# Laying inputs channel-major and weights in 4 KB pieces, without input transposes on TensorE

## The chip, the cores and the metric

The kernel runs on one core of a Trainium2 chip. The metric is the device time in microseconds (us) of one execution; smaller is better. Of the core's engines, TensorE multiplies matrices (PE in the profile, with its weight loads as PEld), VectorE (DVE) and ScalarE (ACT) work element by element, GpSimd (POOL) does little here, and SyncE (SP) issues nearly all transfers (DMAs).

## The reference

One layer of a decoder trunk, for T = 320 token rows (256 of a prompt, and 8 samples of 8 tokens) of D = 2048 channels:

```
h = RMSNorm(x) * norm_mix_g
B_a, C_a, v_a, glu_a, glu_b, gate_a, gate_b = split(h @ w_in)        # 7 x 2048 columns
y_a = (B_a * causal_conv3(C_a * v_a)) @ w_out_a
u   = glu_a * sigmoid(glu_b)
y_b = silu(LayerNorm(causal_conv31(u) + bias)) @ w_out_b
x   = x + (sigmoid(gate_a) * y_a + sigmoid(gate_b) * y_b) @ w_o
x   = x + (silu(n(x) @ w_gate) * (n(x) @ w_up)) @ w_down             # n: RMSNorm, 5632 hidden columns
y   = RMSNorm(x) * final_norm_g
```

Both convolutions also take past rows (state_conv_a, state_conv_b) for the samples and return the new last rows. All inputs and outputs are float32.

## The kernel before

Activations are held channel-major: a chunk c is a tile of 128 channels by 320 tokens, and there are 16 of them. A weight piece is 512 rows by 256 columns (512 KB, `raw`). It is split into a high part `whi` (a cast to fp32r on ScalarE, L207) and a low part `wlo` (raw minus whi on VectorE, L208); activations have such parts too (`rh`/`rl`, `hh`/`hl`). Each product is three matmuls of 128x320: high by high (L244), high weight by low activation (L245), low weight by high activation (L246). A unit is 256 output columns, so one piece is 4 rows of k times 2 accumulators times 3 = 24 matmuls, and a unit of 2048 rows has four pieces.

The first three units (glu_b, glu_a, glu_b again) run as a group (`run_group`): r counts the four pieces of each unit, m the three units, k the four chunks of a piece. In the group, and in the three units after it, the activation is x times the norm's gain, without the norm's factor per token; the factor `rb` is multiplied in when these accumulators are evicted. `at_start(r, m, k)` says what is issued ahead of which step of the group. `x_chunk` turns the token-major x into chunk c by three transposes on TensorE (`px`), then makes `rh`, `rl` and the plain copy `xc`. `x_squares` and `x_factor` make the norm's factor per token row, and `x_spread` spreads it over the partitions by three small matmuls (`rps`). `x_norm(c)` makes the normalized chunk for the later units, and writes `xc` to a scratch tensor, from which `post_o` reads it again. The parameters are turned by `turn_params` (`pp`), the conv states by `turn_state_b` (`sT`) and `turn_state_a` (`aT`), the new rows on their way out in `post_ga` (`uT`) and `rows_a` (`vT`). Twelve matmuls on zeros (`spin`, L92) run while the first loads arrive.

Order: within each engine and queue instructions run in the order in which they were put there by a scheduler from the program's order; `issue_after` holds an instruction behind another. Weight loads go out four pieces ahead of use into five buffers, splits run one piece ahead in the group and two later (three buffers).

Of the kernel before, what the change touches and what calls it, by code (L numbers as in the profile page):

```python
# [38 lines left out]
def trunk_kernel(ctx: ExitStack, tc: tile.TileContext, a):  # L39
# [33 lines left out]
    xpair, xt = rows3("xt")
    xpv = a["x_prompt"][0].rearrange("(i p) d -> p i d", p=P)

    def load_x(c0, c1, queues):
        hs = slice(c0 * P, c1 * P)
        queues[0].dma_start(out=xpair[:, :, hs], in_=xpv[:, :, hs])
# [3 lines left out]
    nc.gpsimd.memset(xt[2][TS:P, :], 0.0)
# [8 lines left out]
    for _ in range(12):  # L91
        first = te.matmul(o[:, :T], idle[:, 0:P], idle, start=True, stop=True, skip_group_check=True).ins  # L92
# [6 lines left out]
    ac.activation(out=warm, in_=ones[:, 0:1], func=AF.Sigmoid)  # L99

    gmix = const.tile([P, NC], F32, name="gmix")
    with tc.issue_after(first):
        pp = pst("pp")
        te.transpose(out=pp[:, 0:NC], in_=grow, identity=ident[:NC, :NC])
    gm = ve.tensor_copy(out=gmix, in_=pp[:, 0:NC]).ins

    prow = const.tile([P, 5, P], F32, name="prow")
    prm = const.tile([P, 5 * P], F32, name="prm")

    def load_params():  # L110
        with tc.issue_after(last_load[0].ins):
            fetch_params()

    def fetch_params():
        r0 = 16
        for n, rows in (("norm_ffn_g", 16), ("conv_b_bias", 16), ("ln_b_g", 16), ("ln_b_b", 16)):
            nc.sync.dma_start(out=prow[r0 : r0 + rows, 0, :], in_=a[n].rearrange("o (c p) -> (o c) p", p=P))
            r0 += rows
        nc.sync.dma_start(out=prow[0:16, 0, :], in_=a["final_norm_g"].rearrange("(c p) -> c p", p=P))
        nc.sync.dma_start(out=prow[80:128, 0, :], in_=a["conv_a_w"].rearrange("o j (c p) -> (o j c) p", p=P))  # L120
        cbv = a["conv_b_w"].rearrange("o j (c p) -> (o j c) p", p=P)
        nc.sync.dma_start(out=prow[:, 1:4, :], in_=cbv[0:384].rearrange("(t q) p -> q t p", q=P))
        nc.sync.dma_start(out=prow[0:112, 4, :], in_=cbv[384:496])

    def turn_params():
        with tc.issue_after(last_mm[0]):
            pp = pst("pp")
            for t in range(4):
                te.transpose(out=pp[:, t * P : (t + 1) * P], in_=prow[:, t, :], identity=ident)
            ve.tensor_copy(out=prm[:, 0:512], in_=pp)  # L130
            pp = pst("pp")
            last_mm[0] = te.transpose(out=pp[:, 0:112], in_=prow[0:112, 4, :], identity=ident[:112, :112]).ins
            ve.tensor_copy(out=prm[:, 512:624], in_=pp[:, 0:112])
# [39 lines left out]
    last_load = [None]  # L173
    nsplit = [0]

    def load_to(i):
        while nload[0] <= min(i, len(pieces) - 1):
            q = pieces[nload[0]]
            n, nb = q["n"], q["nb"]
            r = wp.tile([P, KP, NB], F32, tag="raw", bufs=RAW_BUFS, name=nm("raw"))  # L180
            step = 2 if nload[0] == 0 else n
            for k in range(0, n, step):
                r0 = (q["k0"] + k) * P
                last_load[0] = nc.sync.dma_start(
                    out=r[:, k : k + step, :nb],
                    in_=q["w"][r0 : r0 + step * P, q["n0"] : q["n0"] + nb].rearrange("(k p) n -> p k n", p=P),
                )
# [4 lines left out]

    def split_to(i):
        while nsplit[0] <= min(i, len(pieces) - 1):
# [6 lines left out]
            if nsplit[0]:  # L201
                split(q, 0, n)
            nsplit[0] += 1

    def split(q, k0, k1):
        ks, nb = slice(k0, k1), q["nb"]
        ac.copy(out=q["hi"][:, ks, :nb], in_=q["raw"][:, ks, :nb])  # L207
        ve.tensor_tensor(  # L208
            out=q["lo"][:, ks, :nb], in0=q["raw"][:, ks, :nb], in1=q["hi"][:, ks, :nb].bitcast(F32), op=ALU.subtract
        )  # L210
# [110 lines left out]
    xc = [None] * NC  # L321
# [4 lines left out]
    def x_chunk(c):  # L326
        px = pst("px")
        with tc.issue_after(last_mm[0]):
            for i, (t0, _) in enumerate(blk):
                last_mm[0] = te.transpose(  # L330
                    out=px[:, t0 : t0 + P], in_=xt[i][:, c * P : (c + 1) * P], identity=ident
                ).ins
        r_hi[c] = slot("rh", F32R)
        r_lo[c] = slot("rl", F32R)
        x_last["ac"] = ac.activation(out=r_hi[c], in_=px[:, :T], func=AF.Copy, scale=g_mix(c)).ins
        x_last["ve"] = ve.scalar_tensor_tensor(
            out=r_lo[c], in0=px[:, :T], scalar=g_mix(c), in1=r_hi[c].bitcast(F32), op0=ALU.mult, op1=ALU.subtract
        ).ins
        xc[c] = slot("xc")
        if c % 2:  # L340
            ve.tensor_copy(out=xc[c], in_=px[:, :T])
        else:
            ac.copy(out=xc[c], in_=px[:, :T])

    def x_squares(q):

        with tc.issue_after(x_last["ve"]), tc.issue_after(x_last["ac"]):
            for i in range(3):
                v = xt[i][:, q * 4 * P : (q + 1) * 4 * P]
                if i == 1:  # L350
                    ve.scalar_tensor_tensor(
                        out=v, in0=v, scalar=1.0, in1=v, op0=ALU.mult, op1=ALU.mult, accum_out=sq4[:, i, q : q + 1]
                    )
                else:
                    ac.activation(out=v, in_=v, func=AF.Square, accum_out=sq4[:, i, q : q + 1])

    def x_factor():
        ve.tensor_reduce(out=ss, in_=sq4, axis=mybir.AxisListType.X, op=ALU.add)
        ve.tensor_scalar(out=ss, in0=ss, scalar1=1.0 / D, scalar2=RMS_EPS, op0=ALU.mult, op1=ALU.add)
        rsqrt(ss, rst, rtmp, (P, 3))  # L360

    def x_spread():
        rps = pst("rps")
        dg = []
        for i in range(3):
            dg.append(slot("dg", shape=(P, P)))
            ve.tensor_scalar(out=dg[i], in0=ident, scalar1=rst[:, i : i + 1], scalar2=None, op0=ALU.mult)
        with tc.issue_after(last_mm[0]):
            for i, (t0, n) in enumerate(blk):
                last_mm[0] = te.matmul(  # L370
                    rps[:, t0 : t0 + n], ones, dg[i][:, :n], start=(i == 0), stop=(i == 2), skip_group_check=True
                ).ins
        ve.tensor_copy(out=rb, in_=rps[:, :T])
# [11 lines left out]
    lnacc = sm.tile([P, T], F32, name="lnacc")  # L385


    mid = []

    def load_states(b):  # L390

        if not mid:
            mid.extend((io.tile([P, 2, D], F32, tag="pair", name=nm("win")), io.tile([P, D], F32, tag="one", name=nm("stb"))))
        sbv = a["state_conv_b"].rearrange("o b j d -> (o b j) d").rearrange("(i r) d -> r i d", i=2)
        with tc.issue_after(last_load[0].ins):
            nc.sync.dma_start(out=stb(b)[:120], in_=sbv[:, :, b * NB : (b + 1) * NB])

    def stb(b):
        return mid[1].rearrange("p (g i n) -> p g i n", g=4, i=2)[:, b % 4]
# [11 lines left out]
    ex = [None] * NC  # L411

    def conv_b_tasks(c, up):
# [4 lines left out]
        def first():  # L418
            w = mid[0][:, c % 2, : (T // SS) * 40].rearrange("p (g k) -> p g k", k=40)
# [37 lines left out]
    def turn_state_b(c):  # L457
        pt = pst("sT")
        with tc.issue_after(last_mm[0]):
            for i in range(2):  # L460
                last_mm[0] = te.transpose(  # L461
                    out=pt[:, i * 120 : (i + 1) * 120], in_=stb(c // 2)[:120, i, (c % 2) * P : (c % 2 + 1) * P], identity=ident[:120, :120]
                ).ins
        ex[c] = slot("ext", shape=(P, SB, WB - 1))
        ac.copy(out=ex[c], in_=pt[:, 0:240].rearrange("p (b j) -> p b j", b=SB))

# [562 lines left out]
```

## Time and profile before

| | |
|---|---|
| median of 3 runs | 2098.7 us (2097.35 to 2098.91) |
| profiled execution, its own time | 2099.18 us |
| its span, first to last instruction | 2097.4 us |
| mean granted TensorE clock | 0.999 |
| TensorE busy | 2085.0 us |
| VectorE, ScalarE, GpSimd busy | 1268.7, 822.7, 6.0 us |
| transfers | 323.81 MB, mean 154 GB/s |

In a row of the timeline stand start, duration, engine, line, operation, written tile <- read tiles, shapes, count, and in brackets the idle time before it and what ended it. In the chain stand start, the time that the step takes on the chain, and engine, tile and line. A row of groups ends with total busy us, mean ns of one, and the idle time before them. A row of windows has the stretch, then per engine the busy us and the instructions, then the granted clock, the DMA share and GB/s. TensorE's matmuls are pipelined, so that their durations overlap: what one costs is the distance of two starts.

### The profile page before, as it was taken

The page shows a single profiled execution, that of the slowest core. Times are in us where ns is not written, and L with a number is a line of the kernel's source. Part 1 is how long each engine was busy: PE and PEld are TensorE (multiplying, and loading weights), DVE is VectorE, ACT ScalarE, POOL GpSimd, SP SyncE. Part 2 cuts the span into 40 slices and gives each one's busy share as a digit, 9 for nine tenths or more (in the row PEclk, how much of TensorE's full clock was granted, in tenths as well). Part 3 has the DMA queues.
Part 4 walks back from the last instruction along what each step waited for, and adds up shares of the span by engine and source line. Part 5 has one row for each costly group of instructions (what it writes and reads, how often), then busy time and mean ns, then how long its engine had stood idle before and what let it go on. Part 6 is the DMA issues. An engine that isn't in the chain of part 4 may idle for free.

```text
span 2097.4 us, 34309 instructions
## 1 busy us (share of the span) xinstructions
PE 2085.0 (99%) x14245; PEld 2080.9 (99%) x14245; DVE 1268.7 (60%) x1859; ACT 822.7 (39%) x1245; POOL 6.0 (0%) x24
## 2 busy tenths in 40 slices
PE   9999999999999999999999999999999999999998
PEld 8999999999999999999999999999999999999998
DVE  6888789988987754335555654455333545544444
ACT  5544444444434444333344333333223333333443
POOL 0000000000000000000000000000000000000000
PEclk9999999999999999999999999999999999999999
DMA  8654544444444444444455444444444444444443
GB/s 245 191 167 151 181 150 148 149 149 150 152 151 149 144 153 149 151 151 151 154 173 170 148 150 151 151 151 146 146 155 153 148 149 150 151 151 146 149 141 111
DMA packets 321289, 323.81 MB, mean 154 GB/s; under 512 B 11134, under 2 KB 318862, under 8 KB 321102
## 3 DMA queue, kind: packets, MB, share of 16 engines
q1 hardware_dynamic: 321022, 321.56, 48.1%
q8 instruction: 111, 1.82, 0.3%
q14 instruction: 44, 0.36, 0.0%
q10 hardware_dynamic: 112, 0.07, 0.0%
HBM read 315.42 MB, written 7.60 MB: 154 GB/s over the span
## 4 chain that ended last, share of the span: by engine, by line
PE 99%; DVE 0%; ACT 0%; DMA 0%; issue 0%; SPq 0%; ACTq 0%; DVEq 0%
PE acc L244 32%; PE acc L246 32%; PE acc L245 32%; PE acc L797 0%; PE acc L795 0%; PE acc L796 0%; PE ya L750 0%; DMA raw<-in_w_in 0%; PE px L330 0%; ACT whi L207 0%; PE sT L461 0%; PE acc L801 0%; PE acc L800 0%; DVE wlo L208 0%; PE uT L477 0%
## 5 line engine op out<-in xcount | busy, mean ns | idle before, releaser
L208 DVE TENSOR_TENSOR wlo<-raw,whi 128x1024 fp32r<-128x1024 f32 (+1 forms) x593 | 716.4, 1208 | 713.3 <-ACT whi L207 710.0
L207 ACT CAST whi<-raw 128x1024 fp32r<-128x1024 f32 (+1 forms) x593 | 614.4, 1037 | 1157.1 <-PE acc L245 896.8
L244 PE MATMUL acc<-hh,whi 128*128 128x320 f32 x1600 | 495.2, 310 | 0.0
L246 PE MATMUL acc<-hh,wlo 128*128 128x320 f32 x1600 | 494.5, 309 | 0.0
L245 PE MATMUL acc<-hl,whi 128*128 128x320 f32 x1600 | 494.3, 309 | 0.0
L245 PE MATMUL acc<-gl,whi 128*128 128x320 f32 x1408 | 435.3, 309 | 0.0
L244 PE MATMUL acc<-gh,whi 128*128 128x320 f32 x1408 | 435.1, 309 | 0.0
L246 PE MATMUL acc<-gh,wlo 128*128 128x320 f32 x1408 | 435.1, 309 | 0.0
L245 PEld LDWEIGHTS acc<-hl,whi 128*128 128x128 f32 x1600 | 300.3, 188 | 0.1
L244 PEld LDWEIGHTS acc<-hh,whi 128*128 128x128 f32 x1600 | 300.2, 188 | 0.2
L246 PEld LDWEIGHTS acc<-hh,wlo 128*128 128x128 f32 x1600 | 300.2, 188 | 0.1
L433 DVE SCALAR_TENSOR_TENSOR cb<-win,prm,cb 128x320 f32<-128x320 f32 x480 | 259.4, 549 | 9.1 <-ACT cb L429 1.0
L245 PEld LDWEIGHTS acc<-gl,whi 128*128 128x128 f32 x1408 | 264.3, 188 | 0.1
L246 PEld LDWEIGHTS acc<-gh,wlo 128*128 128x128 f32 x1408 | 264.3, 188 | 0.1
L244 PEld LDWEIGHTS acc<-gh,whi 128*128 128x128 f32 x1408 | 264.3, 188 | 0.0
L246 PE MATMUL acc<-fh,wlo 128*128 128x320 f32 x660 | 204.4, 310 | 0.0
L244 PE MATMUL acc<-fh,whi 128*128 128x320 f32 x660 | 204.1, 309 | 0.0
L245 PE MATMUL acc<-fl,whi 128*128 128x320 f32 x660 | 203.9, 309 | 0.0
L244 PEld LDWEIGHTS acc<-fh,whi 128*128 128x128 f32 x660 | 123.9, 188 | 0.0
L246 PEld LDWEIGHTS acc<-fh,wlo 128*128 128x128 f32 x660 | 123.9, 188 | 0.0
L245 PEld LDWEIGHTS acc<-fl,whi 128*128 128x128 f32 x660 | 123.9, 188 | 0.0
L244 PE MATMUL acc<-ah,whi 128*128 128x320 f32 x256 | 79.3, 310 | 0.0
(187 smaller groups left out, 2105.0 us busy)
## 6 DMA issues: line engine op xcount, KB each, us to landing
raw<-in_w_in SPq DMA_DIRECT2D x223, 512.0 KB, 3.5
raw<-in_w_gate SPq DMA_DIRECT2D x88, 512.0 KB, 3.5
raw<-in_w_up SPq DMA_DIRECT2D x88, 512.0 KB
raw<-in_w_down SPq DMA_DIRECT2D x80, 512.0 KB, 3.3
raw<-in_w_out_a SPq DMA_DIRECT2D x32, 512.0 KB
raw<-in_w_out_b SPq DMA_DIRECT2D x32, 512.0 KB, 3.3
raw<-in_w_o SPq DMA_DIRECT2D x32, 512.0 KB, 3.3
raw<-in_w_down SPq DMA_DIRECT2D x16, 256.0 KB, 2.8
```

The costliest lines, as they stand in the source:

```text
L207: ac.copy(out=q["hi"][:, ks, :nb], in_=q["raw"][:, ks, :nb])
L208: ve.tensor_tensor(out=q["lo"][:, ks, :nb], in0=q["raw"][:, ks, :nb], in1=q["hi"][:, ks, :nb].bitcast(F32), op=ALU.subtract)
L244: te.matmul(o, wh, hi[kk], start=(kk == 0), stop=False)
L245: te.matmul(o, wh, lo[kk], start=False, stop=False)
L246: return te.matmul(o, wl, hi[kk], start=False, stop=(kk == nk - 1)).ins
L433: ve.scalar_tensor_tensor(out=o, in0=win[0][:, :, j + 2 : j + 10], scalar=w_cb(j, c), in1=o, op0=ALU.mult, op1=ALU.add)
```

## The change

Before the launch, numpy now lays x, the parameters and the conv states channel-major, with the norm's gain in front of the first chunk (`lead`), and the weights so that each of a piece's 128 partitions reads one run of 4 KB where it read four of 1 KB. Two outputs leave the core channel-major and are laid out by numpy afterwards. All transposes of inputs on TensorE are gone, and those of the new conv rows; the transposes of y at the end stay. The scratch copy of x is gone: `post_o` reads the input again. The squares of the first norm are taken per chunk on ScalarE, summed over the 16 chunks on GpSimd (`lnacc`), and one matmul with ones sums over the partitions and gives every partition the sum; the factor is then computed on 128x320 tiles, with ScalarE's square root and VectorE's reciprocal. The first weight piece comes in three transfers, two of them on ScalarE's queue; the second is split in halves. Nine matmuls on zeros remain.

```
-    for _ in range(12):
+    for _ in range(9):
         first = te.matmul(o[:, :T], idle[:, 0:P], idle, start=True, stop=True, skip_group_check=True).ins
...
+    lead = const.tile([P, NC + T], F32, name="lead")
+    gmix, xc[0] = lead[:, 0:NC], lead[:, NC : NC + T]
+    sp.dma_start(out=lead, in_=a["x"][:, 0 : NC + T])
+    def load_x(cs):
+        for c in cs:
+            xc[c] = slot("xc")
+            sp.dma_start(out=xc[c], in_=xcol(c))
...
-            step = 2 if nload[0] == 0 else n
...
+            ks = (0, 1, 2, n) if nload[0] == 0 else (0, n)
+            for k, k1 in zip(ks, ks[1:]):
+                eng = aq if nload[0] == 0 and k < 2 else sp
+                dm = eng.dma_start(out=r[:, k:k1, :], in_=q["w"][q["n0"] // NB, :, q["k0"] + k : q["k0"] + k1, :])
...
     def x_chunk(c):
-        px = pst("px")
-        with tc.issue_after(last_mm[0]):
-            for i, (t0, _) in enumerate(blk):
-                last_mm[0] = te.transpose(
-                    out=px[:, t0 : t0 + P], in_=xt[i][:, c * P : (c + 1) * P], identity=ident
-                ).ins
...
+        x_last["ac"] = ac.activation(out=r_hi[c], in_=xc[c], func=AF.Copy, scale=g_mix(c)).ins
         x_last["ve"] = ve.scalar_tensor_tensor(
+            out=r_lo[c], in0=xc[c], scalar=g_mix(c), in1=r_hi[c].bitcast(F32), op0=ALU.mult, op1=ALU.subtract
         ).ins
+    def x_square(c):
+        q = slot("sq")
+        ac.activation(out=q, in_=xc[c], func=AF.Square)
+        if c == 0:
+            nc.gpsimd.tensor_copy(out=lnacc, in_=q)
         else:
+            nc.gpsimd.tensor_tensor(out=lnacc, in0=lnacc, in1=q, op=ALU.add)
     def x_factor():
+        p = pst("rps")
         with tc.issue_after(last_mm[0]):
+            last_mm[0] = te.matmul(p[:, :T], ones, lnacc, start=True, stop=True).ins
+        ve.tensor_scalar(out=lnv, in0=p[:, :T], scalar1=1.0 / D, scalar2=RMS_EPS, op0=ALU.mult, op1=ALU.add)
+        ac.activation(out=lnr, in_=lnv, func=AF.Sqrt)
+        ac.activation(out=warm, in_=lnr[:, 0:1], func=AF.Sigmoid)
+        ve.reciprocal(out=rb, in_=lnr)
+        ve.tensor_tensor(out=lnt, in0=lnv, in1=rb, op=ALU.mult)
+        ve.scalar_tensor_tensor(out=lnt, in0=lnt, scalar=-0.5, in1=rb, op0=ALU.mult, op1=ALU.mult)
+        ve.scalar_tensor_tensor(out=rb, in0=lnt, scalar=1.5, in1=rb, op0=ALU.add, op1=ALU.mult)
     def x_norm(c):
-        with tc.issue_after(last_load[0].ins):
-            nc.sync.dma_start(out=xs[c], in_=xc[c])
...
-                pt = pst("uT")
-                te.transpose(out=pt[: WB - 1 + TS, 0:P], in_=up[:, TP - (WB - 1) : T], identity=ident)
-                ac.copy(out=uo[:, j * P : (j + 1) * P], in_=pt[: WB - 1 + TS, 0:P])
+                nc.sync.dma_start(out=a["nb_new"][c], in_=up[:, TP - (WB - 1) : T])
...
+        elif 3 * r + m <= 7:
+            x_square(6 * r + 2 * m - 2 + k // 2 if k % 2 == 0 else 14 + k // 2)
...
+        elif (r, m, k) == (2, 2, 3):
+            x_factor()
...
+    load_x((1, 2, 3))
+    split_to(0)
+    after_load[1, 0] = lambda: load_x((4, 5))
+    after_load[2, 0] = lambda: load_x((6, 7))
```

Three places show what moves. The first is the start of SyncE's queue. `xt` are the token-major x tiles, `raw` a weight piece, `lead` and `xc` chunks of x. Before:

```order
L78 DMA xt_76<-in_x_prompt 128x2x256
L184 DMA raw_133<-in_w_in 128x2x256
L78 DMA xt_76<-in_x_prompt 128x2x256
L79 DMA xt_77<-in_x_sample 64x256
L184 DMA raw_133<-in_w_in 128x2x256
L184 DMA raw_138<-in_w_in 128x4x256
L184 DMA raw_140<-in_w_in 128x4x256
L78 DMA xt_76<-in_x_prompt 128x2x512
```

And now:

```order
L77 DMA lead<-in_x 128x336
L85 DMA xc_108<-in_x 128x320
L85 DMA xc_110<-in_x 128x320
L85 DMA xc_112<-in_x 128x320
L155 DMA raw_114<-in_w_in 128x512
L155 DMA raw_127<-in_w_in 128x1024
L85 DMA xc_129<-in_x 128x320
L85 DMA xc_131<-in_x 128x320
L155 DMA raw_133<-in_w_in 128x1024
```

Two chunks of x now stand behind each whole piece, and the first half of the first piece (`raw_114`) has moved to ScalarE's queue.

The second is TensorE's queue in the ninth piece of the group (r = 2, m = 2), where the norm's sum is made. `acc` is an accumulator, `rps` the sum's tile, `dg` the factors on a diagonal. Before:

```order
L244 MATMUL acc_132<-rh_368,whi_553 128x320
L245 MATMUL acc_132<-rl_369,whi_553 128x320
L246 MATMUL acc_132<-rh_368,wlo_554 128x320
L370 MATMUL rps_610<-dg_611,ones 128x128
L370 MATMUL rps_610<-dg_613,ones 128x128
L370 MATMUL rps_610<-dg_615,ones 128x64
L244 MATMUL acc_131<-rh_398,whi_553 128x320
```

And now:

```order
L229 MATMUL acc_126<-rl_367,whi_492 128x320
L230 MATMUL acc_126<-rh_366,wlo_493 128x320
L329 MATMUL rps_553<-lnacc,ones 128x320
L228 MATMUL acc_125<-rh_385,whi_492 128x320
L229 MATMUL acc_125<-rl_386,whi_492 128x320
```

One matmul on GpSimd's sum stands in the place of three on VectorE's factors, six matmuls of the stream further down.

The third is ScalarE's queue ahead of that piece's cast (`whi_553` before, `whi_492` now). Before:

```order
L207 CAST whi_487<-raw_324 128x1024
L335 ACTIVATE rh_501<-px_497,gmix 128x320
L343 COPY xc_505<-px_497 128x320
L335 ACTIVATE rh_523<-px_519,gmix 128x320
L355 ACTIVATE xt_76,sq_117<-xt_76 128x512
L355 ACTIVATE xt_77,sq_117<-xt_77 128x512
L207 CAST whi_553<-raw_380 128x1024
```

And now:

```order
L188 CAST whi_448<-raw_301 128x1024
L320 ACTIVATE sq_468<-xc_149 128x320
L313 ACTIVATE rh_477<-xc_257,lead 128x320
L320 ACTIVATE sq_489<-xc_207 128x320
L320 ACTIVATE sq_502<-xc_255 128x320
L320 ACTIVATE sq_511<-xc_209 128x320
L320 ACTIVATE sq_520<-xc_257 128x320
L188 CAST whi_492<-raw_345 128x1024
```

The last four squares (`sq`), each of which GpSimd adds in turn, stand together there, where two sums over token rows stood.

More of the change, by code (lines that the diff above doesn't have):

```diff
@@ L98, in trunk_kernel @@
     warm = const.tile([P, 1], F32, name="warm")
[L99 to L107, printed above, removed]
     prm = const.tile([P, 5 * P], F32, name="prm")
@@ L111, in load_params @@
         with tc.issue_after(last_load[0].ins):
[L112 to L125, printed above, removed]
-        with tc.issue_after(last_mm[0]):
[L127 to L133, printed above, removed]
+            nc.sync.dma_start(out=prm[:, 0:624], in_=a["prm"])
     def col(i):
@@ L200, in split_to @@
             q["hi"], q["lo"] = h, l
-            if nsplit[0]:
+            if nsplit[0] == 1:
+                split(q, 0, 2)
+                split(q, 2, 4)
+            elif nsplit[0]:
                 split(q, 0, n)
@@ L205, in split, with hi_part, lo_part @@
     def split(q, k0, k1):
[L206 to L210, printed above, removed]
+        hi_part(q, k0, k1)
+        lo_part(q, k0, k1)
+    def hi_part(q, k0, k1):
+        ks = slice(k0, k1)
+        if q is pieces[0] and k0 == 0:
+            return ve.tensor_copy(out=q["hi"][:, ks, :], in_=q["raw"][:, ks, :]).ins
+        return ac.copy(out=q["hi"][:, ks, :], in_=q["raw"][:, ks, :]).ins
+    def lo_part(q, k0, k1):
+        ks = slice(k0, k1)
+        return ve.tensor_tensor(
+            out=q["lo"][:, ks, :], in0=q["raw"][:, ks, :], in1=q["hi"][:, ks, :].bitcast(F32), op=ALU.subtract
+        ).ins
     late = []
@@ L320, in trunk_kernel @@
     rb = sm.tile([P, T], F32, name="rb")
-    xc = [None] * NC
+    lnacc = sm.tile([P, T], F32, name="lnacc")
+    lnv = sm.tile([P, T], F32, name="lnv")
+    lnr = sm.tile([P, T], F32, name="lnr")
+    lnt = sm.tile([P, T], F32, name="lnt")
     x_last = {}
@@ L357, in x_factor @@
-    def x_factor():
[L358 to L367, printed above, removed]
-        with tc.issue_after(last_mm[0]):
[L369 to L373, printed above, removed]
+    def x_square(c):
[3 more added lines that the diff above has]
+            nc.gpsimd.tensor_copy(out=lnacc, in_=q)
+        else:
+            nc.gpsimd.tensor_tensor(out=lnacc, in0=lnacc, in1=q, op=ALU.add)
@@ L383, in trunk_kernel @@
     acts_h = lambda: (h_hi, h_lo)
-    lnacc = sm.tile([P, T], F32, name="lnacc")
-    mid = []
+    win_ = [None]
+    ex = [None] * NC
     def load_states(b):
[L392 to L399, printed above, removed]
+        if win_[0] is None:
+            win_[0] = io.tile([P, 2, D], F32, tag="pair", name=nm("win"))
+        for c in (2 * b, 2 * b + 1):
+            ex[c] = slot("ext", shape=(P, SB, WB - 1))
+            with tc.issue_after(last_load[0].ins):
+                nc.sync.dma_start(out=ex[c], in_=a["sb"][c])
     def states_through():
         with tc.issue_after(last_load[0].ins):
-            nc.sync.dma_start(out=a["new_b_s"][0, :, 0 : WB - 1 - SS, :], in_=a["state_conv_b"][0, :, SS : WB - 1, :])
-    w_in = a["w_in"][0]
+            nc.sync.dma_start(out=a["nb_old"], in_=a["state_conv_b"][0, :, SS : WB - 1, :])
+    w_in = a["w_in"]
     O_B, O_C, O_V, O_GA, O_GB, O_SA, O_SB = (i * D for i in range(7))
@@ L455, in post_gb @@
         return f
[L457 to L465, printed above, removed]
     def post_ga(b, raw):
         def f(acc):
-            uo = slot("uo", shape=(WB - 1 + TS, NB))
             for j in range(2):
@@ L1018 @@
     arrays, args = {}, {}
-    for name in _INS:
-        x = _np.ascontiguousarray(inputs[name])
+    for name, x in _lay_in(_np, inputs).items():
         arrays[f"in_{name}"] = x
```

223 lines of the change are left out of this document (84 added, 139 removed).

## The prediction

> **What bounds the kernel now.** I read the busy line and the chain of the page first.
>
> ```profile
> PE 2085.0 (99%) x14245; PEld 2080.9 (99%) x14245; DVE 1268.7 (60%) x1859; ACT 822.7 (39%) x1245; POOL 6.0 (0%) x24
> PE 99%; DVE 0%; ACT 0%; DMA 0%; issue 0%; SPq 0%; ACTq 0%; DVEq 0%
> ```
>
> TensorE is busy in 2085 of 2097.4 us and is 99% of the chain. Work taken off another engine is worth nothing by itself; what counts is TensorE time removed, or TensorE gaps. So next come the shares of the chain over the first 300 us, which hold nearly all transposes that the change touches.
>
> ```profile
> by line: PE acc L246 29.9%; PE acc L244 29.8%; PE acc L245 29.7%; DMA raw<-in_w_in 1.6%; PE px L330 1.3%; ACT whi L207 1.2%; PE sT L461 1.1%; DVE wlo L208 0.8%; issue 0.6%; PE uT L477 0.6%; DVE rl L336 0.4%; ACT rh L335 0.3%; SPq L78 0.3%;
> ```
>
> Of 300 us the transposes of x (px) hold 3.9 us, of the conv state (sT) 3.3, of u (uT) 1.8. About 5% is no matmul: the head, and one stall. TensorE's timeline gives the price of one transposed chunk:
>
> ```profile
> 20.18 0.31 PE L246 MATMUL acc<-rh,wlo 128*128 128x320 f32 x1
> 20.33 0.49 PE L330 MATMUL px<-ident,xt 128*128 128x128 f32 x3
> 20.58 0.39 PE L244 MATMUL acc<-rh,whi 128*128 128x320 f32 x1
> 20.81 0.30 PE L245 MATMUL acc<-rl,whi 128*128 128x320 f32 x1
> ...
> 21.39 0.31 PE L246 MATMUL acc<-rh,wlo 128*128 128x320 f32 x1
> 21.53 0.31 PE L244 MATMUL acc<-rh,whi 128*128 128x320 f32 x1
> ```
>
> Undisturbed matmuls start 0.146 us apart (20.81 to 21.39 is four steps of 0.145); their 0.31 us overlap. From 20.33 to 20.81 stand one matmul and three transposes: 0.48 - 0.146 = 0.33 us for a chunk. The last row is the first matmul of the fourth weight piece: 72 main matmuls are over at 21.53. The stall:
>
> ```profile
> 43.30 0.31 PE L246 MATMUL acc<-rh,wlo 128*128 128x320 f32 x1
> 46.08 0.85 PE L370 MATMUL rps<-dg,ones 128*128 128x128 f32 x6 [2.47 <-DVE dg L367]
> 46.74 0.44 PE L244 MATMUL acc<-rh,whi 128*128 128x320 f32 x1
> 46.98 0.47 PE L245 MATMUL acc<-rl,whi 128*128 128x320 f32 x1
> ...
> 50.18 0.40 PE L245 MATMUL acc<-rl,whi 128*128 128x320 f32 x1
> 50.42 0.31 PE L246 MATMUL acc<-rh,wlo 128*128 128x320 f32 x1
> ```
>
> TensorE waits 2.47 us for the small vector chain of the first norm, and then runs 14 matmuls at 0.27 us apart, about half speed, until 50.42.
>
> **The change, part by part.**
>
> *The norm stall.* 43.30 to 50.42 is 7.12 us and holds 15 matmul steps, 15 x 0.146 = 2.2 us: it costs 4.9. The new x_factor puts one fp32 matmul of ones with lnacc there. The same form stands later in the chain, at 0.54 us:
>
> ```profile
> 658.49 0.54 PE mu L588 x2
> ```
>
> If lnacc is ready, 4.9 - 0.5 = 4.4 us are saved. Its readiness is the question of the GpSimd adds, below.
>
> *Transposes after the fourth piece.* Eight of the sixteen x chunks are turned there: 8 x 0.33 = 2.7 us. sT 3.3 and uT 1.8 go wholly (rows above). The parameters and the state of mixer A:
>
> ```profile
> 51.16 0.44 PE pp L129 x4
> 51.60 0.10 PE pp L132
> 263.70 0.22 PE aT L511 x2
> ```
>
> That is 0.54 + 0.22; the three vT transposes I put at uT's 1.8/16 = 0.1 each. Sum 8.9 us, all on the path, since TensorE is the chain. The evictions that go with them (ACT and VectorE) and the 16 scratch writes by SP gain nothing: nobody on the path waits for them. New on SP are 16 stores of `up`, where loads queue behind a wait for VectorE instead of ACT; the loads have cover, since their wait is for free buffers:
>
> ```profile
> SPq L184 <- DVE wlo L208: 1347.0, 451, 7.4
> DMA packets 321289, 323.81 MB, mean 154 GB/s; under 512 B 11134, under 2 KB 318862, under 8 KB 321102
> ```
>
> Those rows also value the 4 KB pieces at nothing after the head: weights wait for room, not TensorE for weights, and 154 GB/s are used where the head below moves 300. Were that cover gone, a late load would cost its lateness. The other queue edits go with it: one load of parameters for eight, sixteen of states for eight, one of mixer A's state for sixteen, one store of its new rows for six; all on SP, between weight loads that wait for room.
>
> *The head.* Its limits are the transfers.
>
> ```profile
> 0.00:4.00 4.00, 2.75 (x10) 2.75 (x11) 0.33 (x1) 1.49 (x2) 2.64 (x8) 1.00 0.41 131
> 4.00:8.00 4.00, 3.35 (x16) 2.08 (x15) 1.42 (x3) 1.47 (x3) 0.00 (x0) 1.00 1.07 307
> 8.00:12.00 4.00, 3.69 (x23) 2.80 (x21) 2.63 (x6) 3.05 (x7) 0.00 (x0) 1.00 1.08 319
> 6.94 0.56 PE L244 MATMUL acc<-rh,whi 128*128 128x320 f32 x2 [0.29 <-ACT rh L335]
> 7.67 0.62 ACT L207 CAST whi<-raw 128x512 fp32r<-128x512 f32 x1 [0.79 <-DMA raw<-in_w_in]
> ```
>
> The last two columns are DMA share and GB/s: saturated from 4 us on, at 307 to 319 GB/s, after 0.52 MB by 4 us. The second half of the first piece ends 1.18 MB of issues; those bytes have moved at 4 + 0.66/0.307 = 6.1 us, and its user starts at 7.67: 1.5 us of lag. Now the new order. Ahead of the second piece's end stand lead 0.17, three chunks 0.49, and two pieces 1.05: 1.71 MB, moved at 7.9, landed at 9.4. It is split in halves; ACT takes 0.62 (row above) and VectorE about 0.6 for one, so its low part allows the third matmul at 10.7 and the piece ends 22 x 0.146 later, at 13.9. The third piece ends 2.57 MB: moved at 10.7, landed 12.2, then whi and wlo:
>
> ```profile
> L208 DVE TENSOR_TENSOR wlo<-raw,whi 128x1024 fp32r<-128x1024 f32 (+1 forms) x593 | 716.4, 1208 | 713.3 <-ACT whi L207 710.0
> L207 ACT CAST whi<-raw 128x1024 fp32r<-128x1024 f32 (+1 forms) x593 | 614.4, 1037 | 1157.1 <-PE acc L245 896.8 <-issue 233.7 <-ACT win L426 5.8
> L672 DVE SCALAR_TENSOR_TENSOR gl<-x,prm,gh 128x320 fp32r<-128x320 f32 x16 | 8.7, 545 | 0.0
> L671 ACT ACTIVATE gh<-x,prm 128x320 fp32r<-128x320 f32 x16 | 8.9, 558 | 0.0
> L675 ACT ACTIVATE sq<-x 128x320 f32<-128x320 f32 x16 | 7.3, 457 | 0.0
> L312 DVE TENSOR_TENSOR lnacc<-lnacc,sq 128x320 f32<-128x320 f32 x43 | 21.0, 488 | 1.3
> L82 POOL MEMSET xt<- 64x2048 f32 x1 | 1.8, 1800 | 0.3 <-POOLq L1017 0.3
> L99 ACT ACT_TABLE_LOAD x1 | 1.3, 1283 | 1.8 <-issue 1.8
> L847 DVE RECIPROCAL rst<-rtmp x3: 149/155/157, 2084.9 to 2091.3; 128x1 f32<-128x1 f32 x2, 64x1 f32<-64x1 f32 x1
> 1.25 3.57 PE L92 MATMUL spin<-idle 128*128 128x320 f32 x12 [1.25 <-DVE idle L89]
> 2089.92 0.44 DVE yt L835
> ```
>
> 12.2 + 1.04 + 1.21 = 14.4, and 22 matmuls later, at 17.6, the 72 are done, against 21.53: 3.9 us saved, the four px of that stretch (1.3) among them. The bounds: lead and the first half of the first piece, 0.43 MB, have moved at 3.7 and landed at 5.2, so a first matmul comes at 5.8 behind ACT's 0.56 (now 6.94); if larger descriptors lift the rate so far that TensorE never waits afterwards, 5.8 + 72 x 0.146 = 16.3 and 5.2 are saved; if pieces land as late as now, only the px, 1.3. I take 3.9, by the rates in the rows.
>
> The head's idle time could bring the slow clock: after 2.47 us idle, 14 matmuls lost 0.12 each, 1.7 us. Nine spin matmuls (0.3 each, as twelve take 3.57) end near 4, the first real one comes at 5.8, 1.8 us idle, and most of a slow first piece hides behind the second one's landing; I add nothing. The Trainium skill (TensorE: Matmul & The Clock Gate, Part 1) lets the clock fall after an idle window of some 3.4 us; the 2.47 us above did it already, so the row is what I go by; by the page the head stays fast and the sum is the same.
>
> *GpSimd's sums.* Fifteen adds of 128x320 and a copy. No row shows GpSimd adding; the ends are VectorE's add of this shape, 0.49, and the longest GpSimd instruction shown, a fill of 2048 columns in 1.8. That fill is 0.88 ns a column; times 320 columns and three streams (two read, one written) it gives an estimate of 0.84 us, which I take, as the row is of that engine. The sum's matmul stands behind 210 main matmuls: 17.6 + 138 x 0.146 = 37.8. The last four squares stand together on ACT ahead of the ninth piece's whi, which TensorE needs 18 matmuls earlier, at 35.1; less 1.04 and 1.21 the squares are out by 32.9. Four adds then end at 36.3: 1.5 us to spare, and that cover is gone if an add takes over 1.2. ACT's own load there, 1.04 + 2 x 0.56 + 2 x 0.46 = 3.1 us per piece, fits into 24 x 0.146 = 3.5.
>
> *The factor chain after it.* Five VectorE passes and the root, with two weight splits queued between and then two evictions: 5 x 0.5 + 0.46 + 2 x 1.21 + 1.0 = 6.4 us. The root costs a table load back to the sigmoid, 1.28 us on ACT; the whi behind it waits for a buffer that TensorE frees later. The reciprocal I take as a pass; the row shows only one column, 0.155, no more than other passes of one column. The accumulators are wanted again 78 matmuls after the sum, in 11.4 us: the chain is covered unless the reciprocal takes over 5 us, ten passes.
>
> **Sum.** 4.4 + 8.9 + 3.9 = 17.2 us of the profiled span 2097.4, whose execution took 2099.18; the median of the runs, 2098.7, is 0.5 below that. 2098.7 - 17.2 = **2081.5 us**. The last 7.5 us, from 2089.92 on, are as before.
>
> **Rivals.**
> 1. *VectorE and GpSimd hinder each other.* Per piece VectorE has 1.21 + 2 x 0.545 = 2.3 us of passes over two SBUF operands, GpSimd two adds, 1.7. One after the other that is 4.0 against 3.5, over seven pieces 3.4 us of lag, seen as low weights coming late or the sum late. Gain 17.2 - 3.4: **2084.9**. For it: `rl` now reads x from SBUF, not PSUM. Against: up to a piece of lead. The Trainium skill (SBUF — State Buffer, Who interferes with whom) speaks for it: a VectorE instruction with two SBUF inputs and a GpSimd one that reads SBUF block each other for a whole instruction; no run here shows it yet.
> 2. *The head gains nothing but its px*: transfers are the limit before and after. Gain 14.6: **2084.1**. Against: x no longer comes in front of weights in half-megabyte lumps.
> 3. *Slower*: the same turn-taking with dear adds. Seven pieces offer 24.6 us and VectorE takes 16.1 of them; the lag eats the 17.2 when sixteen adds take 25.7 us, 1.6 each; at 2.0 it is 23.5 of lag and **2105**. That is above the upper end of 1.8 (lag 20.3, 2101.8), and only the lack of a row speaks for it.
> 4. *No change*: adds of 1.6 us, 2098.7.
>
> **How the numbers follow.** Forecast 2079 to 2083: 0.45; rival 1, 2083 to 2088: 0.28; rival 2: 0.15; better than 2079: 0.06; no change 0.03; slower 0.03. A measurement of this kernel tells 0.2%, 4.2 us. The range 2077 to 2088 takes in the two rivals and a dense head. Faster 0.94, same 0.03, slower 0.03.
>
> **What would show it.** Right: no px, sT, uT, vT, aT, pp on TensorE; no gap above 1 us before the sum's matmul near 38 us, and steps of 0.146 after; 72 main matmuls over near 17.6. Wrong: an idle TensorE released by GpSimd's lnacc; `wlo` above 1.21 us while an add runs; `raw` landing later than in the order above; a vector pass of 3 us or more holding `rb`; after 70 us any new wait.

## The result and the profile after

The changed kernel takes **2085.55 us** (median of four runs, 2084.72 to 2086.11), against 2098.22 for before beside it: ratio 0.9940, 95% interval 0.9922 to 0.9957. It is faster by 12.7 us, where 17.2 were forecast. The range on record, 2077 to 2088, holds the time; the likeliest case's own, 2079 to 2083, does not.

From the page of after: the busy line, the chain's shares by engine, the packets.

```profile
PE 2071.0 (99%) x14131; PEld 2068.7 (99%) x14131; DVE 1269.4 (61%) x1832; ACT 814.4 (39%) x1206; POOL 25.7 (1%) x39
PE 98%; DMA 0%; ACT 0%; POOL 0%; DVE 0%; issue 0%; SPq 0%; ACTq 0%; POOLq 0%; DVEq 0%
DMA packets 96995, 321.18 MB, mean 154 GB/s; under 512 B 12840, under 2 KB 19624, under 8 KB 96808
```

TensorE is the limit as before, with 14 us less work; GpSimd, 6.0 us before, now works 25.7. The packets fell to a third, and the mean rate is still 154 GB/s.

TensorE's timeline of after (start, duration, instruction, idle time before it and who ended it) has the head, the two places where the group stalls, and, from the chain, two later landmarks:

```profile
4.37 0.87 PE L228 MATMUL acc<-rh,whi 128*128 128x320 f32 x2 [0.35 <-ACT rh L313]
7.75 0.49 PE L228 MATMUL acc<-rh,whi 128*128 128x320 f32 x2
...
16.59 0.31 PE L228 MATMUL acc<-rh,whi 128*128 128x320 f32 x1
...
27.10 0.31 PE L230 MATMUL acc<-rh,wlo 128*128 128x320 f32 x1
27.71 0.41 PE L228 MATMUL acc<-rh,whi 128*128 128x320 f32 x1 [0.31 <-ACT whi L188]
28.98 0.42 PE L230 MATMUL acc<-rh,wlo 128*128 128x320 f32 x1 [0.71 <-DVE wlo L192]
...
38.32 0.31 PE L230 MATMUL acc<-rh,wlo 128*128 128x320 f32 x1
39.53 0.81 PE L329 MATMUL rps<-lnacc,ones 128*128 128x320 f32 x2 [0.90 <-POOL lnacc L324]
40.31 0.31 PE L229 MATMUL acc<-rl,whi 128*128 128x320 f32 x1
...
643.13 0.54 PE mu L492 x2
2074.59 0.44 DVE yt L739
```

The 73rd main matmul starts at 16.59 (21.53 before). The 2.47 us stall of the first norm is gone; three smaller ones, 1.9 us in all (2.7 with the slower steps around them), stand in its place, released by ScalarE, VectorE and GpSimd. After 39.53 no wait of TensorE shows: from there to the landmarks the steps are before's without the transposes. The ledger, in us:

```
                            before    after   gained   forecast
73rd main matmul starts      21.53    16.59     4.94      3.9
matmul of mu                658.49   643.13    15.36     17.2
last eviction (yt)         2089.92  2074.59    15.33     17.2
span                       2097.4   2082.9     14.5      17.2
```

So the head gave 1.0 more than forecast, the stretch from the 73rd matmul to mu 2.9 less (10.4 against 4.4 + 8.9 = 13.3), and 0.8 went at the very end. The profiled execution was the fastest of the four: its span is 0.9 below that of the median run, and before's profiled one lay above its median, which is why 14.5 shrinks to 12.7 between medians.

What happened between 17 and 40 us is on VectorE, GpSimd and ScalarE of after. VectorE and GpSimd, in the order of their starts (the first row is a `wlo` that began with no add under way):

```profile
14.66 1.21 DVE L192 TENSOR_TENSOR wlo<-raw,whi 128x1024 fp32r<-128x1024 f32 x1
...
17.77 1.01 POOL L324 TENSOR_TENSOR lnacc<-lnacc,sq 128x320 f32<-128x320 f32 x1
17.97 1.90 DVE L192 TENSOR_TENSOR wlo<-raw,whi 128x1024 fp32r<-128x1024 f32 x1
18.86 1.75 POOL L324 TENSOR_TENSOR lnacc<-lnacc,sq 128x320 f32<-128x320 f32 x1
19.79 1.17 DVE L314 SCALAR_TENSOR_TENSOR rl<-xc,lead,rh 128x320 fp32r<-128x320 f32 x1
20.69 1.01 POOL L324 TENSOR_TENSOR lnacc<-lnacc,sq 128x320 f32<-128x320 f32 x1
20.88 1.17 DVE L314 SCALAR_TENSOR_TENSOR rl<-xc,lead,rh 128x320 fp32r<-128x320 f32 x1
21.77 1.01 POOL L324 TENSOR_TENSOR lnacc<-lnacc,sq 128x320 f32<-128x320 f32 x1
21.97 1.90 DVE L192 TENSOR_TENSOR wlo<-raw,whi 128x1024 fp32r<-128x1024 f32 x1
```

The end of the chain that leads to the sum's matmul:

```profile
35.94 1.75 POOL lnacc L324
37.76 1.73 POOL lnacc L324
```

ScalarE:

```profile
26.32 0.39 ACT L383 COPY win<-ext 128x240 f32<-128x240 f32 x1 [4.39 <-DMA ext<-in_sb]
26.62 1.04 ACT L188 CAST whi<-raw 128x1024 fp32r<-128x1024 f32 x1
```

Two things are to be seen. First, VectorE and GpSimd take turns. From 17.77 on, each instruction of that list starts while the other engine is still at work, and ends a fixed time after the other's end. The add at 18.86 ends at 20.61, 0.74 us after the `wlo` beside which it began; the `rl` at 19.79 ends 0.35 after that add; the `wlo` at 17.97 ends 1.09 after the add before it. These three times are the same, within 0.03 us, for every add in the five profiles that have the sums on GpSimd. So a duration of 1.01 or 1.75 for an add, 1.17 for an `rl` or 1.90 for a `wlo` holds a wait for the other engine; with no add under way at their start, a `wlo` takes 1.21 and an `rl` 0.55. An add with VectorE idle does not occur, so its time alone is not measured. From one `wlo` to the next the turns are one `wlo`, two `rl` and three adds: 1.09 + 2 x 0.35 + 3 x 0.74 = 4.0 us, which is the distance of 17.97 and 21.97.

Second, ScalarE stands still for 4.39 us at a copy of the conv state (`win<-ext`) whose first reader starts some 35 us later: the scheduler put it into the group, ahead of a `whi` cast, since it has no operand from the group, and its transfer lands at 26.3.

### The profile page after: what moved, and what is told of

Its sections match the earlier page's. It is cut to its first block, busy times and chain, and to the rows that moved or that the text cites. A ratio compares the mean times of both kernels' runs of the same rounds, so it can differ in the third digit from the quotient of the medians.

```text
span 2082.9 us, 33997 instructions
## 1 busy us (share of the span) xinstructions
PE 2071.0 (99%) x14131; PEld 2068.7 (99%) x14131; DVE 1269.4 (61%) x1832; ACT 814.4 (39%) x1206; POOL 25.7 (1%) x39
## 4 chain that ended last, share of the span: by engine, by line
PE 98%; DMA 0%; ACT 0%; POOL 0%; DVE 0%; issue 0%; SPq 0%; ACTq 0%; POOLq 0%; DVEq 0%
PE acc L228 32%; PE acc L230 32%; PE acc L229 32%; POOL lnacc L324 0%; DMA ext<-in_sb 0%; PE acc L701 0%; PE acc L699 0%; PE acc L700 0%; PE ya L654 0%; ACT whi L188 0%; DVE wlo L192 0%; DMA lead<-in_x 0%; PE acc L705 0%; PE acc L704 0%; ACT rh L313 0%
## 5 line engine op out<-in xcount | busy, mean ns | idle before, releaser
L188 ACT CAST whi<-raw 128x1024 fp32r<-128x1024 f32 (+2 forms) x595 | 614.7, 1033 | 1163.3 <-PE acc L229 918.7
```

What stands on the lines that cost most here:

```text
L188: return ac.copy(out=q["hi"][:, ks, :], in_=q["raw"][:, ks, :]).ins
```

## The experiments

Times are medians of four or five runs (hold_fill: one run). "73rd" is the start of the 73rd main matmul in the profile, "rest" is what was gained on before from there to the last eviction, in us. The ratios' intervals are plus or minus 0.0012 to 0.0017, which comes from the runs of before; the kernels' own runs agree within 1.4 us, most within 1, and their medians are compared directly (before's median moved between 2098.2 and 2099.2 from one set of runs to the next, so that differences of a few tenths are not told apart).

```
kernel          median us  ratio   73rd   last eviction   rest
after            2085.55   0.9940  16.59     2074.59      10.39
after_again      2085.55   0.9939  17.79     2075.38      10.80
after_spin14     2084.90   0.9933  16.58     2074.87      10.10
hold_ext         2085.61   0.9936  18.14     2075.18      11.35
hold_rows        2085.63   0.9936  16.88     2075.48       9.79
vector_sums      2083.87   0.9928  17.39     2073.75      12.03
hold_vector      2082.89   0.9923  17.78     2072.98      13.19
hv_spin11        2082.14   0.9923  16.82     2072.02      13.19
hv_spin14        2081.92   0.9921  16.51     2071.71      13.19
hv14_rows        2082.51   0.9921  17.58     2072.78      13.19
hv14_outs        2082.11   0.9921  16.90     2072.10      13.19
hold_fill        2082.82   -       17.50     2072.70      13.19
hv_transposes    2086.75   0.9945  18.74     2076.55      10.58
```

**Hold the state's copy back.** One edit in conv_b_tasks:

```
-                ac.copy(out=w[:, g0:g1, 8 * i : 8 * i + 8], in_=ub[:, 0 : g1 - g0, :])
-            ac.copy(out=w[:, TP // SS :, 2:32], in_=ex[c])
+                lc = ac.copy(out=w[:, g0:g1, 8 * i : 8 * i + 8], in_=ub[:, 0 : g1 - g0, :])
+            with tc.issue_after(lc.ins):
+                ac.copy(out=w[:, TP // SS :, 2:32], in_=ex[c])
```

> Kernel after, with one edit: the copies of the stored state into win (win<-ext) are put behind the copies of up, so that ScalarE no longer waits for their DMA inside the group. Theory: that wait held back the whi of the sixth split and with it TensorE (gaps of 0.31, 0.71 and some small ones at 27 to 29 us, 1.54 us in all), and it held back the squares, so that GpSimd was late with the sum; expected 2085.5 - 1.5 = 2084.0 us, and 2082.8 if the sum's wait of 0.9 us on GpSimd goes with it. Rival: the whi cast was about to wait for something else at the same place (its raw piece, or VectorE's wlo stretched to 1.9 us), so the gaps stay: 2085.5.

Measured: 2085.61, nothing gained. The stalls at 27 to 29 us and the wait for GpSimd are gone as the theory said, but another came. VectorE of hold_ext, and then TensorE's one wait between 18 us and the sum:

```profile
18.17 1.90 DVE L192 TENSOR_TENSOR wlo<-raw,whi 128x1024 fp32r<-128x1024 f32 x1
19.99 2.24 DVE L314 SCALAR_TENSOR_TENSOR rl<-xc,lead,rh 128x320 fp32r<-128x320 f32 x2
22.16 1.89 DVE L192 TENSOR_TENSOR wlo<-raw,whi 128x1024 fp32r<-128x1024 f32 x1
...
27.24 1.89 DVE L192 TENSOR_TENSOR wlo<-raw,whi 128x1024 fp32r<-128x1024 f32 x1
```

```profile
34.25 0.42 PE L230 MATMUL acc<-rh,wlo 128*128 128x320 f32 x1 [1.29 <-DVE wlo L192]
```

With ScalarE no longer late, the squares and adds come without a pause. VectorE needs 3.99 us from one `wlo` to the next with two `rl` and three adds in turn, and 5.08 with three `rl` and four adds (22.16 to 27.24), where TensorE takes 3.5 for a piece. So the rest is 11.35, 1.8 short of the 13.2 that the best kernels reach. The copy was not the only limit; freeing it showed the one behind it.

**Take the sums on VectorE.** In x_square:

```
-        if c == 0:
-            nc.gpsimd.tensor_copy(out=lnacc, in_=q)
-        else:
-            nc.gpsimd.tensor_tensor(out=lnacc, in0=lnacc, in1=q, op=ALU.add)
+        csum(lnacc, q, c)
```

> Kernel after, with the first norm's channel sums taken by VectorE instead of GpSimd (a copy and 15 adds of 128x320). The copy win<-ext still waits in ScalarE's order. Theory (VectorE and GpSimd hold each other up): wlo back from 1.90 to about 1.21 us, rl from 1.17 to 0.55, an add 0.49 on VectorE instead of 1.0 to 1.75 on GpSimd; the 0.9 us wait of the sum's matmul is gone, so 2085.5 - 1.2 = 2084.3 us. Rival: VectorE, with 3.3 of 3.5 us per piece, becomes the engine that the group waits for: wlo later, 2086 to 2088 us.

> Both edits: win<-ext behind the copies of up, and the channel sums on VectorE. Theory (two separate losses, 1.54 and 1.17 us): 2085.5 - 2.7 = 2082.8 us, no wait of TensorE over 0.3 us between 17 and 60 us. Rival (one loss: with the copy out of the way GpSimd is in time, and the sums on VectorE add nothing): the same as hold_ext alone, within 0.3 us. Second rival (VectorE tight): 1 us or more above hold_ext.

Measured: vector_sums 2083.87, hold_vector (both edits) 2082.89. VectorE of hold_vector, over the same stretch:

```profile
16.27 0.48 DVE L296 TENSOR_TENSOR lnacc<-lnacc,sq 128x320 f32<-128x320 f32 x1
16.67 0.54 DVE L314 SCALAR_TENSOR_TENSOR rl<-xc,lead,rh 128x320 fp32r<-128x320 f32 x1
17.13 0.48 DVE L296 TENSOR_TENSOR lnacc<-lnacc,sq 128x320 f32<-128x320 f32 x1
17.53 0.54 DVE L314 SCALAR_TENSOR_TENSOR rl<-xc,lead,rh 128x320 fp32r<-128x320 f32 x1
18.00 1.22 DVE L192 TENSOR_TENSOR wlo<-raw,whi 128x1024 fp32r<-128x1024 f32 x1
19.13 0.48 DVE L296 TENSOR_TENSOR lnacc<-lnacc,sq 128x320 f32<-128x320 f32 x1
```

All three kinds are back at their short times: two adds, two `rl` and a `wlo` take 2.86 us (16.27 to 19.13), less than `wlo` and `rl` alone took beside GpSimd. VectorE did not become the limit, and TensorE waits nowhere between 17 and 60 us. The sums on GpSimd cost 2.7 us with the copy held back (2085.61 to 2082.89; between the two profiled executions 2.2, of which 1.84 lie behind the 73rd matmul) and 1.7 with it in place (2085.55 to 2083.87); the copy is worth 1.0, but only with them gone (2083.87 to 2082.89).

**What kind of GpSimd work is it?** hold_ext, with fills of a square's tile for chunks 0 to 7 and copies for 8 to 15 in place of the adds (the sum of squares is left out, and a constant stands for it):

```
-        if c == 0:
-            nc.gpsimd.tensor_copy(out=lnacc, in_=q)
-        else:
-            nc.gpsimd.tensor_tensor(out=lnacc, in0=lnacc, in1=q, op=ALU.add)
+        if c < 8:
+            for _ in range(4):
+                nc.gpsimd.memset(q, 0.0)
+        else:
+            nc.gpsimd.tensor_copy(out=slot("sd"), in_=q)
```

> hold_ext, with GpSimd's sums replaced: for chunks 0 to 7 four fills of the square's tile (writes only), for chunks 8 to 15 one copy of the square (one read, one write). The sum of squares itself is left out (lnacc is a constant), so the first norm's factor is not the real one. Theory A (an add of two tiles in SBUF on GpSimd and VectorE's operations with two tiles shut each other out): while GpSimd fills or copies, rl stays at 0.55 us and wlo at 1.21. Theory B (anything that GpSimd does in SBUF slows VectorE): rl 1.1 and wlo 1.9 in both halves, as beside the adds. Between them: 1.21 beside the fills and 1.9 beside the copies would put it on GpSimd's reads.

GpSimd, then VectorE, of hold_fill:

```profile
12.37 10.91 POOL L324 MEMSET sq<- 128x320 f32 x31 [10.37 <-ACT sq L321]
23.23 1.41 POOL L326 COPY sd<-sq 128x320 f32<-128x320 f32 x1
24.89 0.85 POOL L326 COPY sd<-sq 128x320 f32<-128x320 f32 x2
```

```profile
17.13 1.23 DVE L192 TENSOR_TENSOR wlo<-raw,whi 128x1024 fp32r<-128x1024 f32 x1 [0.39 <-ACT whi L188]
18.27 1.05 DVE L315 SCALAR_TENSOR_TENSOR rl<-xc,lead,rh 128x320 fp32r<-128x320 f32 x2
...
23.10 1.23 DVE L192 TENSOR_TENSOR wlo<-raw,whi 128x1024 fp32r<-128x1024 f32 x1 [0.39 <-ACT whi L188]
24.24 0.74 DVE L315 SCALAR_TENSOR_TENSOR rl<-xc,lead,rh 128x320 fp32r<-128x320 f32 x1
```

GpSimd filled without a pause from 12.4 to 23.3 us, and VectorE did not notice: `wlo` 1.23, two `rl` in 1.05. The copies take turns as the adds do: the one at 23.23 ended at 24.63, 0.31 us after the `wlo` beside which it began, and took 1.41, where two others later took 0.85 together; the `rl` that began beside it took 0.74. So theory B falls: it is not GpSimd being busy. Theory A holds but for this: one operand read by GpSimd is enough. Whether a `wlo` is stretched by a copy was not seen, since none had to wait for one by more than 0.06 us. The eight copies cost TensorE nothing: the rest is 13.19, and the time of the one run, 2082.82, is hold_vector's. The Trainium skill (SBUF — State Buffer, Who interferes with whom) says just this: a VectorE instruction with two SBUF inputs contends with a GpSimd one that reads SBUF, not with one that only writes. The rows agree: `wlo` 1.90 beside adds, 1.23 beside fills.

**The head's clock.** after_again is after, unchanged; hv_spin11 and hv_spin14 are hold_vector with another count; after_spin14 is after with 14.

```
-    for _ in range(9):
+    for _ in range(14):
```

> Kernel after, unchanged, on the chip and beside the runs of before that the next three share, and for a second look at how long its head runs at the slow pitch (0.267 us from 4.37 to 7.75 us in the first profile). Expected 0.994 of before. Theory (the slow pitch ends at a moment that does not belong to the program, since hold_ext had it to 10.9 us with the same head and 9 spins): the second profile shows another end, anywhere from 7 to 11 us. Rival (the head of after always ends it at its 12th main matmul, 7.75 us, and hold_ext's order changed it): 7.75 again.

> hold_vector with 11 spins in place of 9, so that they end near 4.6 us and no idle 0.66 us stands between them and the first main matmul at 4.68. Theory (the idle time after the spins keeps TensorE at the slow pitch): main matmuls at 0.147 us from about 5 us on; the first 12 then end near 6.5 and wait for the third slice of the weights (7.8 us), the 72nd ends near 17.1 instead of 17.9, and the time is 0.8 us below hold_vector. Rival (the slow pitch ends at its own moment, whatever the spins do): no change, within 0.4 us.

> hold_vector with 14 spins, which end near 5.5 us if they stay slow, 0.8 us after the first data is there. Theory: as for 11 spins, since the later start of the first 12 main matmuls is made up before the third slice of the weights lands at 7.8 us: 0.8 us below hold_vector. Rival (the head is bound by its first matmul): 0.8 us above it.

> Kernel after with 14 spins in place of 9 and nothing else: GpSimd still takes the sums and win<-ext still waits in ScalarE's order. The 73rd main matmul should start at 16.5 us (16.6 and 17.8 in the two profiles of after). Theory (the rest of the group is paced by VectorE and GpSimd, which hold each other up, so a faster head only makes TensorE wait longer at 28 and 38 us): at most 0.8 us below after's 2085.55, so 2084.7 to 2085.5. Rival (head and group add up, as without the sums on GpSimd, where 14 spins brought 0.97 us): 2084.3 to 2084.6.

TensorE of after_again, then of hv_spin14:

```profile
4.91 0.88 PE L228 MATMUL acc<-rh,whi 128*128 128x320 f32 x2 [0.89 <-ACT rh L313]
9.37 0.66 PE L230 MATMUL acc<-rh,wlo 128*128 128x320 f32 x2
9.87 0.46 PE L228 MATMUL acc<-rh,whi 128*128 128x320 f32 x2
...
17.79 0.31 PE L228 MATMUL acc<-rh,whi 128*128 128x320 f32 x1
```

```profile
1.25 4.10 PE L92 MATMUL spin<-idle 128*128 128x320 f32 x14 [1.25 <-DVE idle L89]
5.15 0.58 PE L228 MATMUL acc<-rh,whi 128*128 128x320 f32 x2
5.57 0.46 PE L229 MATMUL acc<-rl,whi 128*128 128x320 f32 x2
...
16.51 0.31 PE L228 MATMUL acc<-rh,whi 128*128 128x320 f32 x1
36.75 0.70 PE L326 MATMUL rps<-lnacc,ones 128*128 128x320 f32 x2
```

Two matmuls take 0.73 at the slow pitch (0.27 apart) and 0.46 at the fast one. The granted clock of the profile reads 1.00 all through the head, so it is the distance of the starts that shows the pitch, and that a clock is behind it is not shown here. The same kernel left the slow pitch at 7.75 us in one execution and about 9.7 in another: the moment is not the program's. In the seven profiles with 9 spins, which end at 4.0, and then 0.32 to 0.89 us of idle time before the first main matmul, it came at 7.3 (hold_rows) to 10.9 us (hold_ext). In the six with next to no such gap it came earlier: hv_spin11 was fast from about 6.2 us, the four with 14 spins from 5.4 to 5.9, and hv_transposes of the next experiment, which has 9 spins and fills the gap with transposes, from 7.2. The times follow: 0.75 and 0.97 us below hold_vector, as the theory said; that hv_spin14's first matmul starts 0.5 us later costs nothing. The Trainium skill (TensorE: Matmul & The Clock Gate, Part 1) lets the clock rise after some 3.4 us of sustained work, counted in a window that runs free of the kernel; 1.25 to 5.15 us of spins, and the changing moment with a gap, agree with that.

On after itself 14 spins bring 0.65 at most (2084.90, all runs below after_again's except one at 2085.30, but the lowest of after's first four, 2084.72, is below them all). Its head is as early as in the first profile, 16.58, and its rest is shorter, 10.10: a part of what TensorE wins in the head it waits off at 28 and 40 us, since VectorE and GpSimd keep their own pace.

**What a transposed chunk costs.** In x_chunk of hold_vector:

```
+        px = pst("px")
+        with tc.issue_after(last_mm[0]):
+            for i in range(3):
+                last_mm[0] = te.transpose(out=px[:, i * P : (i + 1) * P], in_=ones, identity=ident).ins
```

> hold_vector with three 128x128 transposes per chunk of x put back on TensorE, of constants, into a PSUM tile that nobody reads: the price of px alone, without its reads by ScalarE and VectorE. Theory (the prediction's 0.33 us for three, each of them on the path because TensorE is dense): the 8 in the group's later pieces cost 2.7 us, and those in the head as much again unless the loads cover them: 2085.6 to 2088.2 us. Rival (they fit into TensorE's gaps in the head, and the later 8 beside VectorE's work): within 1 us of hold_vector.

Measured 2086.75: 3.86 us above hold_vector. The rest falls by 13.19 - 10.58 = 2.6 us, eight chunks at 0.33, as forecast; the head loses 0.96 (17.78 to 18.74), far less than eight times 0.33, partly because the extra work left no gap and the pitch was fast from 7.2 us on.

**Does the piece layout matter?** In load_to, and the weights passed as they are:

```
-in_=q["w"][q["n0"] // NB, :, q["k0"] + k : q["k0"] + k1, :]
+in_=q["w"][(q["k0"] + k) * P : (q["k0"] + k1) * P, q["n0"] : q["n0"] + NB].rearrange("(k p) n -> p k n", p=P)
```

> hold_ext, with the weights in the old row layout (each partition reads runs of 1 KB instead of 4 KB of a piece; x stays channel-major). Theory (the head is faster than forecast because 4 KB runs move faster, 402 GB/s against 319 at 8 to 12 us): the 72nd main matmul ends near 20 us instead of 16.6, and the time is 3 to 4 us above hold_ext. Rival (the rate comes from the order and number of the loads, or the engines bind the head): 16.6 us and the time of hold_ext within 0.5 us. After the head neither expects a difference, since a piece is due every 3.5 us.

> hv_spin14 with the weights in the old row layout (runs of 1 KB). In hold_rows VectorE held the group up whatever the loads did, so that a later head could not show; here TensorE is dense from 10 us on. Theory (the piece layout is worth something in the head, where the loads move 355 GB/s instead of 390): the sixth to eighth pieces land up to 2 us later, TensorE waits for whi, and the time is 0.5 to 2 us above hv_spin14. Rival (worth nothing): within 0.2 us of hv_spin14, 2081.9.

hold_rows equals hold_ext, but there VectorE sets the pace. Its 73rd matmul starts at 16.88 us, not near 20, so the theory that the head owes its gain to the long runs falls. On hv_spin14 the row layout's median is 0.6 us higher (2082.15 to 2082.98 against 2081.72 to 2082.08), all of it before the 73rd matmul; the rest is 13.19 in both. But the two were run beside different runs of before, the ratios are both 0.9921, and hv14_outs below, which has pieces, reaches 2082.62. So a cost in time is not shown. In the profile of hv14_rows TensorE waits 1.31 us for the third slice of the first weights, at 8.47 us; but that slice was used at 7.05 to 8.30 us in the kernels with pieces, so one profile can't tell how much of it is the layout. What is shown is the rate: between 8 and 16 us hold_rows and hv14_rows both moved 361 and 355 GB/s, hold_ext 395 and 381, hv_spin14 398 and 386. So pieces give about a tenth more rate in the head; that this is worth time is not shown, and after the head nothing changes.

**The last store.** SyncE waits for the landing of the last stores of y_prompt. The rows give the wait in all, the number of waits and the longest; first before, then after:

```profile
SPq L1025 <- DMA out_y_prompt<-yt: 2.1, 4, 0.6
```

```profile
SPq L954 <- DMA out_y_prompt<-yt: 2.9, 1, 2.9
```

> hv_spin14 with y_prompt and y_sample declared after the other outputs instead of before them, nothing else. It asks why the last store of y_prompt is waited for 2.9 us at the end of every kernel with the new layout, against 2.1 in before. Theory (where y_prompt lies in DRAM sets how evenly the stores are served): another wait, 2.1 to 2.5 us, and a time up to 0.8 us lower. Rival (it comes from how the stores are dealt out to the DMA engines after so many others): 2.9 us, and the time of hv_spin14 within 0.3 us.

Before has four waits, 2.1 us in all, and every kernel with the new layout a single one of 2.7 to 3.0, so the two rows do not compare one store with one store. Both kernels start to issue the last store 3.9 us after the last eviction, so that the 0.8 us between the last eviction and the span in the ledger arises behind that. hv14_outs measured 2082.11, with a wait of 2.8 us: where y_prompt stands among the outputs is not the reason. What is stays open.

## Why the prediction was right, and where it was off

- *The norm's stall and the later transposes, 4.4 + 8.9 = 13.3 us.* Right: with GpSimd's adds and the state's copy out of the way, six profiles give 13.19. In hv_spin14 the sum's matmul starts without a wait (36.75). px came back at 0.33 each.
- *The head, 3.9 us.* 4.94 in the first profile, 3.74 in the second, with two errors against each other. The data came sooner than the sum said: first matmul at 4.37 and not 5.8, and the rate (last column) above the 319 GB/s that the sum went by:

```profile
8.00:12.00 4.00, 4.00 (x29) 4.00 (x28) 2.48 (x6) 2.83 (x6) 0.00 (x0) 1.00 1.04 402
```

  But the slow pitch, which was put at nothing because it would hide behind the second piece, cost about 1.2 us in after_again (17.79, against 16.58 with 14 spins).
- *GpSimd's sums: the step that failed.* The forecast let the adds run beside VectorE: four adds of 0.84 us, with 1.5 us to spare. The size was near, as an add ends 0.74 us after its turn comes; what failed is the overlap. Taking turns with VectorE, the adds took 1.0 to 1.9 us each, and both signs of being wrong came that the prediction had named for it: TensorE idle for lnacc (0.90 us) and `wlo` above 1.21 (1.90). The first rival had the mechanism and should have been the forecast: it was given 0.28, with "up to a piece of lead" against it, while the rows already had VectorE at 2.3 of 3.5 us per piece in passes that a GpSimd add could hold up. Its 2084.9 is 0.65 from the median. That its 4.0 us per piece is also the distance measured in after is chance: it added two adds of 0.84 to 2.3 us, and the profile has three adds of 0.74 and 1.8 us of VectorE. The range holds the time because it took in this rival; the likeliest case did not come.
- *Not foreseen: the copy `win<-ext`.* The prediction priced the loads of states as transfers on SP, and not who would wait for them: ScalarE, inside the group. It has a part in the 2.5 to 2.9 us that the stretch from the 73rd matmul to mu fell short in the two profiles of after: vector_sums, with only this left, has a rest 1.16 short, hold_ext, with only the sums left, 1.84. By the medians the two overlap: over hold_vector stand 1.0 us with only the copy left, 2.7 with only the sums, and 2.7 with both.
- *The end, "as before".* It was 0.8 us longer.
- *The reciprocal.* Taken as a pass, 0.5; it takes 2.15, and the factor is out 7.8 us after the sum's matmul began, not 6.4. As forecast TensorE does not wait for it:

```profile
41.40 2.15 DVE L333 RECIPROCAL rb<-lnr 128x320 f32<-128x320 f32 x1 [0.54 <-ACT lnr L331]
46.84 0.48 DVE L336 SCALAR_TENSOR_TENSOR rb<-lnt,rb 128x320 f32<-128x320 f32 x1
```

- *The second rival* (head gains its px only, 2084.1) came near the time by chance: the 73rd matmul was 3.7 to 4.9 us earlier. The slow cases did not come: the copy and the adds took 1.1 + 20.6 = 21.7 us, where 25.7 was the price of no change. By the sum of those rivals 21.7 would still have cost 13.2 us (16.1 + 21.7 - 24.6), and 2.5 to 2.9 were lost: the measured times of the adds already hold their waits for VectorE, which the sum counts a second time:

```profile
L324 POOL TENSOR_TENSOR lnacc<-lnacc,sq 128x320 f32<-128x320 f32 x15 | 20.6, 1373 | 5.6 <-ACT sq L320 4.6
```

hv_spin14, with the sums on VectorE, the copy held back and 14 spins, takes 2081.92 us, 3.6 below after and 16.4 below before beside it (ratio 0.9921, 0.9908 to 0.9935). It is the fastest version tried, and 0.4 us from the forecast for the change as it was.

## What to carry to other kernels

Moving a small sum to an idle engine is not free when that engine reads the memory that a nearly full engine reads: add both engines' times per stage, as if they took turns, before calling the work covered. When a copy or load loses an operand that held it in place, look where the scheduler now puts it, and who queues behind its wait. And when one stall is taken out and the time stays, measure the stretch between two landmarks: the next limit stands close behind.

## What was not expected of the hardware

- GpSimd's adds of 128x320 and VectorE's passes with two operands in SBUF took strict turns, instruction by instruction: an add ended 0.71 to 0.74 us after the VectorE instruction beside which it began, an `rl` 0.35 and a `wlo` 1.08 after the add. So an add lasted 1.0 to 1.9 us, `wlo` went from 1.21 to 1.90 and `rl` from 0.55 to 1.16. GpSimd's fills did not take part.
- After nine spins and a gap of 0.32 to 0.89 us TensorE ran at about half its pace for another 3.0 to 6.2 us, until a moment that differs from one execution of a kernel to the next, while the granted clock read 1.00.
- VectorE's reciprocal of 128x320 takes 2.15 us, over four times a pass of two operands (0.48).
